# RWKV part of a hybrid layer: pair products in three lumps, filler blocks regrouped, the LoRA's low weights padded to 128 rows, the merge split by branch

## The chip, the cores and the metric

The kernel runs on one core of a Trainium2 chip. The metric is the device time of one execution in microseconds, median over several executions; the kernel before took 1315.39 us (median of 3, 1311.83 to 1317.93).

## The reference

One layer of a diffusion backbone, in fp32, for 512 latent tokens and 128 context tokens (640 in all, model width 1024). After a modulated RMS norm one wide projection gives the inputs of two branches and of two gates:

```python
h = _rmsnorm(x, p["norm1_g"]) * (1.0 + sc1) + sh1
u_rw, u_na, gate_rw, gate_na = jnp.split(h @ p["w_in"], IN_SPLITS, axis=-1)
o_rw, s_new = _rwkv_branch(u_rw, s0, ...)         # RWKV-7, both directions, 8 heads of 64
o_na = _na_latent(q, k, v, ctx_k, ctx_v, rpb)     # 2-D neighbourhood attention (context: plain attention)
merged = (jax.nn.sigmoid(gate_rw) * (o_rw @ p["w_o_rwkv"])
          + jax.nn.sigmoid(gate_na) * (o_na @ p["w_o_na"]))
x = x + g1 * (merged @ p["w_out"])
x = x + g2 * ((jax.nn.silu(h2 @ p["ffn_w1"]) * (h2 @ p["ffn_w3"])) @ p["ffn_w2"])
```

The RWKV branch is a recurrence over tokens, whose step is

```python
sa = jnp.einsum("bhvk,bhk->bhv", s, a)
s = s * w[:, :, None, :] + sa[..., None] * b[:, :, None, :] + v[..., None] * k[:, :, None, :]
y = jnp.einsum("bhvk,bhk->bhv", s, r)
```

with decay `w` and step size `a` made by small two-layer maps (the LoRAs). The outputs are both token groups after the layer, the new states, and the context's keys and values.

## The kernel before

The program runs in stages: modulation and norms; attention's projections and attention itself; the RWKV branch; the output projection; the feed-forward layer. The change touches the RWKV part, from about 285 to 770 us of the profile, and the first matmuls behind it.

**Precision.** A matrix product is done as three passes on TensorE: high weights on high activations, high on low, low on high. `wload` (L138) fetches a weight tile of 512 KB into `wst`, ScalarE casts the high part (`whi`, L149), and DVE or GpSimd subtracts it (`wlo`, L150). `feat_gen` (L158) issues the passes (L165) one after another, each of 128x320.

**Two kinds of work share TensorE.** RWKV is done in chunks of 64 tokens, for four pairs of heads (ct 0 to 3, `c` below), both directions. That work is many small matmuls (64x64 blocks, 32x32 in places) with waits on other engines between them. Into the waits the kernel puts *filler*: the matmuls of large projections that are needed anyway (tile `fl`), one by one from a generator (`stream`, L1264). The filler's units are the columns of the gate projections (`g0` to `g15`, 48 matmuls each), of keys, receptances and values of the next head pair (`k`, `r`, `v`, 48 each), and of the merge (`m0` to `m7`, 42 each: the 128 merged features of both branches, 4 K-tiles of attention and 3 of RWKV). `PRM["order"]` names their order, `wait` the marks that a unit needs. `PRM["plan"]` is a table with one entry per step of the small work: how many filler matmuls go in there, and how many steps of a second and third small generator. `weave` (L1294) reads it. TensorE's order is thus written out by hand; the other engines' order is set by a scheduler.

**One head pair** goes through these steps.
- `main` / `n_job` (L921): products of the chunk's keys and decayed keys (L931), in three groups of chunks (`parts8`: 8, 8 and 4), whose 32x32 corners ScalarE collects in `Nt`.
- `inv` (L1011): DVE transposes them into `RL` (L1015) and inverts 32x32 triangles of all chunks in place, in 30 steps ("hops", s = 1 to 30). A hop is a product into `pr` (L1043) and an add into `RL` (L1047), two of each; the first three and the last three use L1029 and L1036.
- In the hops, nine jobs on TensorE for the three groups, one at each third hop: `g_job` (Grams: 6 matmuls a chunk, into three PSUM buffers; DVE masks them into `AG`, L951, and `TG`, L954), `v_job` (values to token-major, or `flip` from the mirrored chunk, evicted by ScalarE), `t_job` (keys and decayed keys to token-major, two PSUM buffers, ScalarE). The six PSUM buffers with the tag `w` serve all small work in turn.
- Also there: `out` of the head pair before (group norm, with `inv_sqrt_bcast`: L874, DVE L878, GpSimd's power L880, ScalarE's copy L882, transposes L887; then bonus L1188, gate L1193) and `bonus` (L905).
- The blocks that complete 64x64 inverses: L1064 (32x32 matmuls), L1079.
- `carry` (L1088): eight chunks in sequence, three steps each: A (L1110, L1120, L1126), B (L1135, on the copy `x0` that ScalarE makes of A's result), C (L1147, L1151); then DVE makes the next state (L1164). Beside it the preparation of the next head pair (`prep_a`: the LoRA's pair of matmuls, L511 with 128 rows and L513 with 64, and more).

Attention's output `o` was written to DRAM in an earlier stage, the RWKV branch's is written head pair by head pair (L1204); `o_load` (L1212) brings back all seven K-tiles for the merge, 4 + 2 (or 3) K-tiles to a transfer. The merge multiplies by the gates, read back from DRAM (L1227), and sums (L1238, L1240). Its last K-tile, that of head pair 3, is never written: `last_gen` (L1361) multiplies it directly (L1372) and adds (L1373, L1375), and the output projection (`w0`) starts between its steps. The residual input `x2` (L1344) is loaded just before.

## Time and profile before

| | |
|---|---|
| median of 3 executions | 1315.39 us |
| profiled execution | 1312.36 us, its span 1310.5 us |
| TensorE busy | 1252.3 us, 96% of the span |
| DVE busy | 673.3 us, 51% |
| ScalarE, GpSimd busy | 468.1 us, 292.5 us |
| mean granted TensorE clock | 0.972 of 2.4 GHz |
| chain that ended last | TensorE 78%, DVE 13%, DMA 3% |

A profile covers one execution. Matmuls are pipelined, so their rows overlap, and the distance of two starts tells what one costs. The granted clock has two levels, 1.0 and 0.5 of full speed (2.4 and 1.2 GHz). A wait is put down to what came last.

### The profile page before, as it was taken

Reading aid. Unit: us, or ns where it says so; the run is one execution under the profiler, and the core shown is the slowest. Engines: PE = TensorE matmul, PEld = TensorE weight load, DVE = VectorE, ACT = ScalarE, POOL = GpSimd, SP = SyncE. Lnnn points to the kernel's source line nnn. Section 1 sums busy time; section 2 is a strip of 40 time slices with the busy share of each in tenths; the row PEclk is TensorE's granted clock in tenths of the full one; section 3 lists DMA queues with packets and bytes.
Section 4 is the critical chain, followed back from the end, with each engine's and each line's share of the span. In section 5 each row is a group of like instructions: output and inputs, shape, how many; then the busy total and the mean of one; then the engine's idle time right before and its main releaser. Section 6 shows DMA issues by size and latency. Waiting matters only on the chain.

```text
span 1310.5 us, 27065 instructions
## 1 busy us (share of the span) xinstructions
PE 1252.3 (96%) x11418; PEld 1081.0 (82%) x11418; DVE 673.3 (51%) x1458; ACT 468.1 (36%) x961; POOL 292.5 (22%) x292
## 2 busy tenths in 40 slices
...
GB/s 346 147 81 121 284 234 167 123 95 50 70 46 24 99 27 44 47 76 49 55 222 86 164 244 69 100 75 96 65 65 94 67 81 79 67 65 89 73 89 41
DMA packets 52849, 134.87 MB, mean 103 GB/s; under 512 B 6612, under 2 KB 20436, under 8 KB 50680
## 3 DMA queue, kind: packets, MB, share of 16 engines
...
## 4 chain that ended last, share of the span: by engine, by line
PE 78%; DVE 13%; DMA 3%; ACT 2%; issue 2%; POOL 1%; SPq 0%; DVEq 0%; ACTq 0%; POOLq 0%
PE f L165 24%; PE acc L252 21%; PE fl L165 12%; PE mm L165 4%; DVE pr L1043 3%; DVE RL L1047 3%; PE psa L203 2%; PE lg L756 1%; PE pt L704 1%; PE po L763 1%; PE w L1110 1%; DMA o<-o_d 1%; PE lg L755 1%; PE w L1135 1%; DVE AG L951 1%
## 5 line engine op out<-in xcount | busy, mean ns | idle before, releaser
L165 PE MATMUL f<-h,whi 128*128 128x256 f32 (+1 forms) x1408 | 306.3, 309 | 0.6 <-POOL h L155 0.6
L165 PEld LDWEIGHTS f<-h,whi 128*128 128x128 f32 x1408 | 236.6, 189 | 1.1 <-POOL h L155 1.0
L149 ACT CAST whi<-wst 128x1024 fp32r<-128x1024 f32 x126 | 132.0, 1049 | 274.6 <-PE acc L252 106.6
L165 PE MATMUL f<-h,wlo 128*128 128x384 f32 (+1 forms) x704 | 217.7, 309 | 0.0
L150 DVE TENSOR_TENSOR wlo<-wst,whi 128x1024 fp32r<-128x1024 f32 x95 | 117.9, 1243 | 180.1 <-ACT whi L149 180.0
L165 PE MATMUL fl<-h,whi 128*128 128x320 f32 x736 | 188.6, 334 | 0.0
L165 PEld LDWEIGHTS fl<-h,whi 128*128 128x128 f32 x736 | 129.5, 197 | 6.7 <-issue 0.2
L165 PEld LDWEIGHTS f<-h,wlo 128*128 128x128 f32 x704 | 133.0, 189 | 0.0
L165 PE MATMUL fl<-h,wlo 128*128 128x320 f32 x368 | 122.8, 334 | 0.0
L150 POOL TENSOR_TENSOR wlo<-wst,whi 128x1024 fp32r<-128x1024 f32 x31 | 83.6, 2698 | 106.4 <-ACT whi L149 102.7
L252 PE MATMUL acc<-whi,ul 128*128 128x512 f32 (+1 forms) x230 | 88.6, 385 | 0.0
L252 PE MATMUL acc<-whi,uh 128*128 128x512 f32 (+1 forms) x230 | 88.3, 386 | 0.0
L252 PE MATMUL acc<-wlo,uh 128*128 128x512 f32 (+1 forms) x230 | 88.2, 386 | 0.0
L252 PE MATMUL acc<-whi,h 128*128 128x512 f32 x240 | 80.7, 409 | 0.5 <-DVE h L361 0.5
L165 PEld LDWEIGHTS fl<-h,wlo 128*128 128x128 f32 x368 | 72.4, 197 | 3.8
L165 PE MATMUL fl<-o,whi 128*128 128x320 f32 x224 | 58.2, 338 | 14.2 <-DMA o<-o_d 12.6
L165 PE MATMUL mm<-h,whi 128*128 128x320 f32 x256 | 64.4, 329 | 0.0
L1490 DVE SCALAR_TENSOR_TENSOR a<-a,f 128x384 f32<-128x384 f32 (+1 forms) x44 | 21.5, 488 | 69.6 <-PE f L165 69.5
L252 PEld LDWEIGHTS acc<-whi,h 128*128 128x128 f32 x240 | 45.4, 191 | 14.0 <-issue 2.0
L165 PEld LDWEIGHTS fl<-o,whi 128*128 128x128 f32 x224 | 40.2, 200 | 17.0 <-DMA o<-o_d 13.4
L252 PE MATMUL acc<-whi,m 128*128 128x512 f32 x160 | 51.8, 400 | 0.0
L154 ACT CAST uh<-a 128x384 fp32r<-128x384 f32 (+1 forms) x44 | 20.2, 458 | 87.6 <-DVE a L1490 87.6
...
## 6 DMA issues: line engine op xcount, KB each, us to landing
...
```

The source lines that it names most:

```text
L149: act.copy(hi, st)
L150: (eng or dve).tensor_tensor(out=lo, in0=st, in1=hi.bitcast(F32), op=ALU.subtract)
L154: act.copy(hi, src)
L165: pe.matmul(ps[:, :t1 - t0], w[:, a:a + 128], x[:, k0 + kt, t0:t1], start=n == 0, stop=n == 3 * nk - 1)
L203: pe.matmul(ps[32 * j:32 * j + 32, c0:c0 + n], cs[:, kt, :], w[:, j * n:(j + 1) * n], start=kt == 0, stop=kt == 7)
L252: pe.matmul(pss[i][:, a:b], x[:, kt, ts_], w[:, cs_], start=ki == 0 and n == 0, stop=ki == last and n == 2)
L704: pe.transpose(pst[:, c * 128:(c + 1) * 128], L[:, c * 128:(c + 1) * 128], ident)
L755: pe.matmul(psl[:, o_:o_ + n], QS[hd][:, qs], KS[hd][:, k0:k0 + n], start=True, stop=False)
L756: pe.matmul(psl[:, o_:o_ + n], ql[rows, qs], KS[hd][rows, k0:k0 + n], start=False, stop=True)
L1043: dve.tensor_tensor(out=prv, in0=V(RL[:, s + 1 + a, :], [[32, b - a], [0, s]], s), in1=V(RL[:, s, :], [[0, b - a], [1, s]]), op=ALU.mult)
L1047: dve.tensor_tensor(out=dst, in0=dst, in1=prv, op=ALU.add)
L1490: dve.scalar_tensor_tensor(out=a, in0=a, scalar=0.5, in1=p3[:, :n], op0=ALU.mult, op1=ALU.mult)
```

## The change

- The nine jobs become three lumps, at hops 2, 9 and 16: each does the value, the transpose and the Gram job of one group.
- `plan` is new. The three groups of `n_job` run without filler between them, and filler goes in fewer, larger blocks. In `carry` none stands between steps A and B (the second of three places), 9 matmuls after B and 6 after C.
- The merge's units are split: `a0` to `a7` (attention's 4 K-tiles, 24 matmuls) and `b0` to `b7` (RWKV's 3, 18 matmuls), each with its own weight load of 512 or 384 columns and its own gate load (`merge_load`), in two buffers. `b` waits for the mark O2, `a4` to `a7` for the end of ct 3's `main`. `o_load` makes one transfer per K-tile.
- The LoRA's low weights lie in one persistent tile `UL` with zeros in the other 64 rows, so that L513's successor multiplies 128 rows.
- `inv_sqrt_bcast` yields once more between power and copy, and `out` may go on while `main` runs.

Outside the RWKV part TensorE's matmuls stand in the same order as before. The number of filler matmuls is 1440 in both, the number of uninterrupted blocks of them in the region 172 before and 105 now (counted in TensorE's order). The diff, cut:

```diff
@@ -26,40 +26,40 @@
 TCARGS = dict(schedule_with_timeline_sim=True)
 
 PRM = dict(
-    order=("g2 k1 g3 r1 g4 v1 g5 k2 g6 r2 g7 g8 v2 g9 k3 g10 r3 g11 v3 g12 g13 g14 g15 m0 m1 m2 m3 m4 m5 m6 "
-           "m7"),
+    order=("g2 k1 g3 r1 g4 g5 v1 g6 g7 k2 r2 g8 g9 v2 g10 g11 k3 r3 g12 g13 v3 g14 g15 a0 a1 a2 a3 a4 a5 a6 a7 "
+           "b0 b1 b2 b3 b4 b5 b6 b7"),
...
-        "16 2 2 2 6",
-        "0.0.0 6.0.1 5.0.1 4.0.1 5.0.1 5.0.0 5.1.0 5.0.0 5.1.0 4.0.0 5.1.0 5.0.0 5.1.0 5.0.0 4.1.0 5.0.0 "
-        "5.1.0 5.0.0 5.1.0 4.0.0 5.1.0 5.0.0 5.1.0 5.0.0 5.1.0 4.0.0 5.1.0 5.0.0 5.1.0 5.0.0 4.1.0 5.0.0 "
-        "8.1.0 8.0.0 7.1.0 4.0.0 4.1.0 4.0.0",
-        "9.0 4.1 4.1 5.1 4.1 5.1 4.1 4.1 5.1 4.1 4.1 5.1 4.1 4.1 5.1 4.1 5.1 4.1 4.1 5.1 4.1 4.1 5.1 4.1 4.1 "
-        "7.1",
...
+        "28.0 0.0 0.0 0.0 0.0",
+        "0.0.0 13.0.1 3.0.0 11.0.0 4.0.0 4.0.1 3.0.1 4.0.1 4.0.0 3.0.0 11.0.0 4.0.0 3.0.0 4.0.0 4.0.0 3.0.0 "
+        "4.0.0 11.0.0 4.0.0 3.0.0 4.0.0 4.0.0 3.0.0 4.0.0 3.0.0 4.0.0 4.0.0 3.0.0 4.0.0 4.0.0 3.0.0 4.0.0 "
+        "9.0.0 7.0.0 8.0.0 0.0.0 7.0.0 0.0.0",
+        "10.0 0.0 9.2 6.2 0.0 9.2 6.2 0.0 9.2 6.2 0.0 9.2 6.2 0.0 9.2 6.2 0.0 9.2 6.2 0.0 9.2 6.2 0.0 9.2 6.2 "
         "6.0",
...
+        "24.2 0.0 0.0 0.0 0.0",
+        "0.0.0 19.1.1 0.1.0 0.0.0 0.1.0 0.1.1 0.1.1 0.1.1 0.1.0 0.1.0 0.0.0 2.0.0 2.1.0 2.1.0 7.1.0 7.1.0 "
+        "7.1.0 7.0.0 7.0.0 7.0.0 7.0.0 7.0.0 7.0.0 7.0.0 7.0.0 7.0.0 7.0.0 7.0.0 7.0.0 7.0.0 7.0.0 7.0.0 "
+        "11.0.0 9.0.0 10.0.0 0.0.0 9.0.0 0.0.0",
+        "10.0 0.0 9.0 6.0 0.0 9.0 6.0 0.0 9.0 6.0 0.0 9.0 6.0 0.0 9.0 6.0 0.0 9.0 6.0 0.0 9.0 6.0 0.0 9.0 6.0 "
+        "6.0",
...
-    h3=1, h4=1.07, g1=2)
+    jobs=(2, 9, 16), h3=1, h4=1.07, g1=2)
...
@@ -143,11 +143,12 @@
             rot.append(rot.pop(0))
         pl, nst, nhl = rot[-1] if rot else wpool[-1]
         st = pl.tile([P, 1024], F32, tag="wst", bufs=nst, name=nm("wst"))
-        sp.dma_start(st if len(src.shape) == 2 else V(st[:, :], [[128, 8], [1, 128]]), src)
+        n = src.shape[1] if len(src.shape) == 2 else 1024
+        sp.dma_start(st[:, :n] if len(src.shape) == 2 else V(st[:, :], [[128, 8], [1, 128]]), src)
         hi = pl.tile([P, 1024], F32R, tag="whi", bufs=nhl, name=nm("whi"))
         lo = pl.tile([P, 1024], F32R, tag="wlo", bufs=nhl, name=nm("wlo"))
-        act.copy(hi, st)
-        (eng or dve).tensor_tensor(out=lo, in0=st, in1=hi.bitcast(F32), op=ALU.subtract)
+        act.copy(hi[:, :n], st[:, :n])
+        (eng or dve).tensor_tensor(out=lo[:, :n], in0=st[:, :n], in1=hi[:, :n].bitcast(F32), op=ALU.subtract)
         return hi, lo
...
@@ -414,6 +415,10 @@
     kt_ = kp.tile([P, NT], F32, tag="kt", bufs=1, name="kt_")
     vp0 = kp.tile([P, NT], F32, name="vp0")
 
+    UL = kp.tile([P, 2, 2, 128], F32R, name="UL")
+    for d in range(2):
+        pool.memset(UL[64 - 64 * d:128 - 64 * d, d].bitcast(F32), 0.0)
+
     def pre_t():
         return kp.tile([P, 643], F32, tag="pre", bufs=4, name=nm("pre"))[:, :NT]
 
-        S.ul = kp.tile([P, 2, 128], F32R, tag="ul", bufs=1, name=nm("ul"))
+        S.ul = UL
         act.copy(V(S.uh[:, 0, :], [[1, 512]]), upw[:, 0:512])
         for d in range(2):
             rr = hrows[d]
-            pool.tensor_tensor(out=S.ul[rr], in0=V(upw[rr, :], [[256, 2], [1, 128]], 128 * d),
+            pool.tensor_tensor(out=UL[rr, d], in0=V(upw[rr, :], [[256, 2], [1, 128]], 128 * d),
                                in1=V(S.uh[rr, d, :], [[256, 2], [1, 128]]).bitcast(F32), op=ALU.subtract)
 
     def parts(ct, k):
...
-                    pe.matmul(ps[:, :H2], S.ul[drows, wi, :], x[drows, hf * H2:(hf + 1) * H2],
+                    pe.matmul(ps[:, :H2], S.ul[:, d, wi, :], x[:, hf * H2:(hf + 1) * H2],
...
                               op1=ALU.add)
             pool.tensor_tensor(out=r, in0=r, in1=mhalf[:, :10], op=ALU.pow)
             yield
+            yield
             act.copy(c64(sqt), V(r[:, :], [[1, 10], [0, 64]]))
             yield
             pa, pb = ps_(), ps_()
...
-        jobs = {2 + 3 * i: (f, l) for i, (f, l) in enumerate(
-            (f, l) for l in parts8 for f in (g_job, v_job, t_job))}
+        jobs = dict(zip(PRM["jobs"], parts8))
...
-                    jobs[s][0](S, *jobs[s][1])
+                    for f in (v_job, t_job, g_job):
+                        f(S, *jobs[s])
                 yield
...
-            for t, t_d in zip(o, o_d):
-                sp.dma_start(t.bitcast(F32)[:, a:b, :], t_d[a:b, :, :].rearrange("q p t -> p q t"))
+            for q in range(a, b):
+                for t, t_d in zip(o, o_d):
+                    sp.dma_start(t.bitcast(F32)[:, q, :], t_d[q])
...
-        def mt_load(c8):
-            ts_ = pre_t(), pre_t()
-            for t, src in zip(ts_, (tna_d, trw_d)):
-                sp.dma_start(t, src[c8])
-            return ts_
-
-        def merge_gen(c8, w):
-
-            mt.append(mt_tile(c8))
-            ta, tr = mt_load(c8)
+        def merge_load(g, i):
+
+            k0, k1, src = (0, 4, tna_d) if g == "a" else (4, 7, trw_d)
+            w = wload(w_o[i][:, 128 * k0:128 * k1], pool)
+            t = sb.tile([P, NT], F32, tag="mx", bufs=2, name=nm("mx"))
+            sp.dma_start(t, src[i])
+            return w, t
+
+        def merge_gen(g, c8, wt):
+
+            w, t = wt
+            if g == "a":
+                mt.append(mt_tile(c8))
+            k0, nk = (0, 4) if g == "a" else (4, 3)
             for (a, b) in halves:
-                for (t, out_, nk, k0) in ((ta, mt[c8], 4, 0), (tr, tr, 3, 4)):
-                    ps = flps()
-                    yield from feat_gen(ps, w, o, nk, a, b, wcol=128 * k0, k0=k0)
-                    dve.scalar_tensor_tensor(out=out_[:, a:b], in0=t[:, a:b], scalar=1.0, in1=ps[:, :b - a],
-                                             op0=ALU.add, op1=ALU.mult)
-                pool.tensor_tensor(out=mt[c8][:, a:b], in0=mt[c8][:, a:b], in1=tr[:, a:b], op=ALU.add)
+                ps = flps()
+                yield from feat_gen(ps, w, o, nk, a, b, k0=k0)
+                dve.scalar_tensor_tensor(out=(mt[c8] if g == "a" else t)[:, a:b], in0=t[:, a:b], scalar=1.0,
+                                         in1=ps[:, :b - a], op0=ALU.add, op1=ALU.mult)
+                if g == "b":
+                    pool.tensor_tensor(out=mt[c8][:, a:b], in0=mt[c8][:, a:b], in1=t[:, a:b], op=ALU.add)
 
         def unit(g):
+
             i = int(g[1:])
-            if g[0] == "m":
-                return w_o[i], lambda w: merge_gen(i, w)
+            if g[0] in "ab":
+                return 24 if g[0] == "a" else 18, lambda: merge_load(g[0], i), lambda w: merge_gen(g[0], i, w)
             if g[0] == "g":
-                return w_rw[15 + i], lambda w: gate_gen(i, w, flps, sb, "fl")
+                return 48, lambda: wload(w_rw[15 + i], pool), lambda w: gate_gen(i, w, flps, sb, "fl")
             ci, dst = {"k": (4 + i, kt_), "r": (i, rt_), "v": (8 + i, v)}[g[0]]
-            return w_rw[ci], lambda w: proj_gen(ci, dst, flps, kp, "pre", 4, w)
+            return 48, lambda: wload(w_rw[ci], pool), lambda w: proj_gen(ci, dst, flps, kp, "pre", 4, w)
...
-        wait.update({f"m{i}": "O2" if i < 4 else "I3" for i in range(8)})
+        wait.update({f"a{i}": "A3" for i in range(4, 8)})
+        wait.update({f"b{i}": "O2" for i in range(8)})
...
-                        if i + 1 < len(order) and order[i + 1] == "m0":
-                            o_load(0, 4)
-                            o_load(4, 7 if "O2" in marks else 6)
+                        if i + 1 < len(order) and order[i + 1] == "a0":
+                            o_load(0, 6)
+                            if "O2" in marks:
...
-                weave(main(ct, S))
+                weave(main(ct, S), (og,))
+                marks.add(f"A{ct}")
```

On TensorE, at ct 1's `n_job` (`fl` is filler; lines of the second piece are those of the changed file: L931 is L936 there, L165 is L166), before:

```order
L165 MATMUL fl_4439<-h_85,whi_4173 128x320
L931 MATMUL w_4466<-AG,f_706_4380 32x64 x32
L165 MATMUL fl_4439<-h_86,whi_4173 128x320
L165 MATMUL fl_4439<-h_85,wlo_4174 128x320
L931 MATMUL w_4502<-AG,f_715_4432 32x64 x32
L165 MATMUL fl_4439<-h_85,whi_4173 128x320
L165 MATMUL fl_4439<-h_86,whi_4173 128x320
L931 MATMUL w_4538<-AG,f_706_4380 32x64 x8
L931 MATMUL w_4538<-AG,f_715_4432 32x64 x8
L165 MATMUL fl_4439<-h_85,wlo_4174 128x320
```

and now:

```order
L166 MATMUL fl_4528<-h_85,whi_4352 128x320
L936 MATMUL w_4546<-AG,f_696_4325 32x64 x32
L936 MATMUL w_4580<-AG,f_712_4424 32x64 x32
L936 MATMUL w_4614<-AG,f_696_4325 32x64 x8
L936 MATMUL w_4614<-AG,f_712_4424 32x64 x8
L166 MATMUL fl_4528<-h_86,whi_4352 128x320
L166 MATMUL fl_4528<-h_85,wlo_4353 128x320
```

The two filler blocks between the three groups are gone; behind them 16 filler matmuls stand in one block, and then the first lump.

On DVE, in ct 1's inverse (L1043 and L1047 are the hops; L951, L954 the masks of the first group's Grams), before:

```order
L1047 TENSOR_TENSOR RL_4566<-RL_4566,pr_4581 128x12x8
L1043 TENSOR_TENSOR pr_4581<-RL_4566 128x99 x2
L1047 TENSOR_TENSOR RL_4566<-RL_4566,pr_4581 128x11x9
L951 TENSOR_TENSOR AG<-w_4593,K 64x8x64 x2
L954 TENSOR_TENSOR TG<-w_4594,K 128x8x64
L1047 TENSOR_TENSOR RL_4566<-RL_4566,pr_4581 128x11x9
L954 TENSOR_TENSOR TG<-w_4595,K 128x8x64
```

and now (L956 and L959 are the masks, L1047 and L1051 the hops):

```order
L1047 TENSOR_TENSOR pr_4654<-RL_4632 128x119 x2
L1051 TENSOR_TENSOR RL_4632<-RL_4632,pr_4654 128x7x17 x2
L956 TENSOR_TENSOR AG<-w_4716,K 64x8x64 x2
L1047 TENSOR_TENSOR pr_4654<-RL_4632 128x108
L1047 TENSOR_TENSOR pr_4654<-RL_4632 128x126
L959 TENSOR_TENSOR TG<-w_4717,K 128x8x64
L959 TENSOR_TENSOR TG<-w_4718,K 128x8x64
L1051 TENSOR_TENSOR RL_4632<-RL_4632,pr_4654 128x6x18
```

The masks of the first Gram stood behind the hop of width 9 and stand behind the hop of width 17 now.

On SyncE's queue, at the end of the RWKV part (L1344 is `x2`, L146 a weight load, L1366 the gates for `last_gen`), before:

```order
L1227 DMA pre_8993<-tna_d 128x640
L1227 DMA pre_8994<-trw_d 128x640
L1344 DMA x_0_9112<-in_xs_dram 128x1024
L1344 DMA x_1_9113<-in_xs_dram 128x1024
L1344 DMA x_2_9114<-in_xs_dram 128x1024
L1344 DMA x_3_9115<-in_xs_dram 128x1024
L1344 DMA x_4_9116<-in_xp_dram 128x1024
L146 DMA wst_9130<-in_w_o_dram 128x8x128
L1227 DMA pre_9050<-tna_d 128x640
L1366 DMA tr_9158<-trw_d 128x640
L1366 DMA tr_9160<-trw_d 128x640
```

and now (L1359, L147, L1381 in the same roles; L1235 is `merge_load`):

```order
L147 DMA wst_9185<-in_w_o_dram 128x8x128
L1235 DMA mx_9001<-trw_d 128x640
L147 DMA wst_9191<-in_w_out_dram 128x1024
L1235 DMA mx_9067<-trw_d 128x640
L1381 DMA pre_9205<-trw_d 128x640
L1381 DMA pre_9207<-trw_d 128x640
L1381 DMA pre_9209<-trw_d 128x640
L147 DMA wst_9555<-in_w_out_dram 128x1024
L147 DMA wst_9603<-in_w_out_dram 128x1024
L1381 DMA pre_9211<-trw_d 128x640
L1359 DMA x_0_9167<-in_xs_dram 128x1024
L1359 DMA x_1_9168<-in_xs_dram 128x1024
```

The loads of `w_o`, of the first tile of `w_out` and of four gates stand ahead of `x2` now.

## Rows read from the trace of the kernel before

**Rows 1.** Stretches: length, busy time of PE, PEld, DVE, ACT, POOL; clock, DMA:
```profile
297.00:340.00 43.00, 42.45 (x811) 38.30 (x801) 38.94 (x133) 18.27 (x36) 18.31 (x16) 1.00 0.18 57
...
393.00:443.50 50.50, 46.80 (x845) 41.71 (x844) 42.96 (x141) 21.75 (x44) 15.02 (x18) 1.00 0.16 52
...
509.00:562.50 53.50, 47.98 (x837) 43.21 (x836) 40.84 (x140) 21.93 (x44) 14.90 (x17) 0.94 0.18 60
...
620.50:684.00 63.50, 47.99 (x805) 42.00 (x803) 41.68 (x142) 17.79 (x33) 17.67 (x13) 0.82 0.40 143
```

**Rows 2.** TensorE's waits, 285 to 770 us: total, times, longest:
```profile
PE fl L165 <- DMA o<-o_d: 12.6, 3, 5.8
PE w L887 <- ACT pre L882: 5.7, 4, 2.1
...
PE fl L1372 <- DVE pre L1373: 4.0, 1, 4.0
```

**Rows 3.** TensorE in time, filler (start, length, instruction):
```profile
290.30 0.46 PE L165 MATMUL fl<-h,whi 128*128 128x320 f32 x2
...
290.74 0.46 PE L165 MATMUL fl<-h,whi 128*128 128x320 f32 x2
...
447.18 0.73 PE L165 MATMUL fl<-h,whi 128*128 128x320 f32 x2
...
447.98 0.73 PE L165 MATMUL fl<-h,whi 128*128 128x320 f32 x2
```

**Rows 4.** TensorE in time, ct 3's carry:
```profile
715.51 0.45 PE L1120 MATMUL w<-ZV,K 64*64 64x64 f32 x8
715.79 0.40 PE L1126 MATMUL w<-R__2920,ZV 64*64 64x64 f32 x8
716.12 0.42 PE L165 MATMUL fl<-o,wlo 128*128 128x320 f32 x1
...
716.91 0.45 PE L1135 MATMUL w<-x,Rt 64*64 64x64 f32 x8
```

**Rows 5.** TensorE in time, ct 1's carry, a LoRA pair:
```profile
468.54 0.31 PE L511 MATMUL w<-lx,uh 128*128 128x320 f32 x1
...
469.13 0.69 PE L1147 MATMUL w<-ZV,TG 128*64 128x64 f32 x16
```

**Rows 6.** TensorE in time, ct 0's last chunk, steps A and B without filler:
```profile
388.32 0.45 PE L1126 MATMUL w<-R__2920,ZV 64*64 64x64 f32 x8
388.80 0.45 PE L1135 MATMUL w<-x,Rt 64*64 64x64 f32 x8
```

**Rows 7.** DVE in time, ct 1's inverse:
```profile
398.67 1.25 DVE L1015 STREAM_TRANSPOSE RL<-Nt 128x1024 f32<-128x1024 f32 x1 [3.01 <-ACT Nt L934]
...
405.41 1.39 DVE L951 TENSOR_TENSOR AG<-w,K 64x512 f32<-64x512 f32 x2
...
414.70 0.46 DVE L1043 TENSOR_TENSOR pr<-RL 128x112 f32<-128x112 f32 x2
...
415.47 0.47 DVE L1043 TENSOR_TENSOR pr<-RL 128x120 f32<-128x120 f32 x2
```

**Rows 8.** Further stretches, columns as in rows 1:
```profile
443.00:446.40 3.40, 3.40 (x86) 3.16 (x85) 3.33 (x7) 1.42 (x4) 1.76 (x2) 1.00 0.19 44
446.40:449.80 3.40, 3.40 (x18) 3.07 (x18) 1.48 (x4) 1.90 (x4) 1.15 (x1) 0.50 0.36 139
...
508.90:512.50 3.60, 3.60 (x165) 2.95 (x164) 0.00 (x0) 2.14 (x2) 1.55 (x1) 1.00 0.37 123
```

**Rows 9.** The chain of waits, 650 to 690 us (start, length, piece):
```profile
659.50 9.86 DMA o<-o_d
```

**Rows 10.** The end of the RWKV part, engines in time:
```profile
739.32 0.77 PE L887 MATMUL w<-K,pre 128*128 128x128 f32 x5 [0.16 <-ACT pre L882]
...
744.37 2.32 DVE L155 TENSOR_TENSOR o<-out,o 128x320 fp32r<-128x320 f32 x1
```

**Rows 11.** The chain of waits, 740 to 790 us:
```profile
769.34 0.60 DVE pre L1373 x2
```

37 lines of the change are left out of this document (15 added, 22 removed).

## The prediction

> **What bounds the kernel now.** I read the page first, then the RWKV part by stretches, then TensorE's waits there, then TensorE and DVE row by row. TensorE is the engine to watch: in ct 1's `n_job` and inverse it is busy 46.80 of 50.50 us [rows 1]. The exception is ct 3, 47.99 of 63.50 us at a mean clock of 0.82 [rows 1], where filler waits 12.6 us for `o` to come back from DRAM [rows 2]. The other waits are short: 5.7 us for the copy in `out`'s inverse square root, 4.0 us at the first matmul of the last step [rows 2]. So two things can move the time: what TensorE's own instructions cost, and the waits.
>
> A filler matmul costs 0.147 us in a run of its kind: three from 290.30 to 290.74. At the lower clock it is 0.267: 447.18 to 447.98 [rows 3]. A block of filler costs more than its matmuls. In `carry` four fill 716.12 to 716.91, 0.79 us instead of 0.59, so 0.20 is paid where 64-row work follows. The eight small matmuls ahead take 0.33 us to the filler (715.79 to 716.12), where eight of that kind before small work take 0.28 [rows 4]: 0.05 more. A block between small matmuls thus costs 0.25 us beside its work.
>
> **The change part by part.**
>
> *Filler blocks.* 172 become 105, with 1440 matmuls in both. 67 x 0.25 = 16.8 us less. Where 128-row work follows, the surcharge should be smaller. No row here isolates it; with 0.10, half the smaller value, 67 blocks give 6.7, and with 0.30 they give 20.1. I take 0.25, from the row.
>
> *LoRA.* A pair takes 468.54 to 469.13, 0.59 us [rows 5]. The second matmul has 64 rows and is followed by small work. With 128 rows both run at filler's pace and only one switch is left, 0.147 + 0.147 + 0.20 = 0.49. 24 pairs x 0.10 = 2.4 us less. From both sides: nothing gained, or, if the switch hides, 24 x 0.30 = 7.1. The Trainium skill ("TensorE: Matmul & The Clock Gate", Step-by-step: what each phase is for) says that the time goes by the columns streamed, not by the rows. By it 128 rows would save nothing and the sum would be 2.4 us smaller. The row's pair costs twice what two 320-column matmuls cost in a run, which speaks for a cost of the switch that this rule does not name.
>
> *No filler between steps A and B.* I cost it at nothing. B waits for the copy `x0` of A's first matmuls, and the matmuls L1120 and L1126 of A still cover it: in ct 0's last chunk, without filler, B starts 0.48 us after the start of the last eight of A, whose length is 0.45 [rows 6]. If ScalarE is late, each of 32 chunks pays: 0.3 us each would be 10 us. The 9 and 6 filler matmuls in the other two places cover B's copies and DVE's new state, 1.3 and 0.9 us where before four or five matmuls gave 0.6 to 0.7; what waits for the state they save I leave out.
>
> *Lumps.* This is the part that adds waits. A lump takes all six `w` buffers, and the next user of a buffer waits until the masks have run; DVE has them later in its order. In ct 1, `RL` begins at 398.67, and the first Gram's masks began 6.7 us later, behind hop 9 [rows 7]. A hop costs 0.77 there (414.70 to 415.47), so the eight hops to the 17th add 6.2, and the masks take 1.39 [rows 7]: they now end 14.3 us after the start of `RL`, which itself waits for ScalarE's copy of `n_job`. TensorE has until there 38 filler matmuls (5.6 us), the first lump, and a bonus, two steps of `out` and three blocks' surcharges (about 1.7, at 0.147 and 0.25). A lump is 192 instructions as the trace counts them (an fp32 matmul twice), and 165 such ran in 3.60 us [rows 8], so 4.2 us. That is 11.5 of 14.3, and TensorE waits about 3 us. The second lump waits in the same way, for buffers that `bonus` and `out` hold until hops 23 to 26 are through: I take 5 more. So 8 us in ct 1 and in ct 2, and 6 in ct 0, where no `out` stands between. Before, the stretches had 0.6, 3.7 and 5.5 us without a matmul in ct 0, 1 and 2 [rows 1]. That is 5.4 + 4.3 + 2.5 = 12.2 more. In return `out`'s inverse square root has one more step and more filler to hide in, so two of its four waits go, 3.6 of the 5.7 us [rows 2]. Net +8.6. Bounds: nothing, if the filler covers the masks; 24 if the waits are twice as long.
>
> *ct 3.* The `o` loads are asked for as 12 transfers instead of 4, one K-tile each, and early filler (`a0`) needs the first K-tiles alone. Before, a transfer of 9.86 us ended the wait [rows 9], and the RWKV K-tile of ct 2 came after it; `a` units don't need that one. I let 5 of 12.6 us stand. On the other side the second bonus waits behind all hops of ct 3 with almost no filler ahead of it, about 12 us, since the attention units come after it. `out`'s longest wait, 2.1 us [rows 2], goes. Before, 15.5 us of the stage had no matmul, and a mean clock of 0.82 means 23 us at the lower level, part of them idle [rows 1]: some 24 us lost in all. I set 18 now: 6 less. Bounds: all 24 stay, or 10 more go with the second bonus.
>
> *The end.* Before, all filler left over ran after the last gate, and covered what leads from `out`'s transposes to the last step, 739.32 to about 745 [rows 10]. Now nothing is left there: 5.6 us with 1.1 us of work, a wait of 4.5. What it replaces is as long: TensorE waited 4.0 us [rows 2], since DVE had `w_out` ahead of it and started the step at 769.34 [rows 11]. On SyncE that weight now stands ahead of `x2`. I take +0.5. The last step itself is bound by DVE in both.
>
> *Clock and the rest.* Falls after the 32x32 blocks, as from 446.40 [rows 8], cost 3.4 us x (1 - 0.147 / 0.267) = 1.5 each; I let one stand per head pair, about as many as now. The weights of the merge come in smaller pieces on SyncE and GpSimd, of the same bytes: nothing.
>
> Sum: -16.8 - 2.4 + 8.6 - 6 + 0.5 = -16.1 us. Against the profiled execution, 1312.36, whose span is 1310.5, that is 1296.3. The median shown, 1315.39, lies 3.0 above that execution; I forecast 1299 for a median.
>
> **The rivals.**
>
> *The waits eat it.* If lumps wait so much longer that they cost 12.2 more, and ct 3 keeps its 24 us (6 more), the sum is +2.1: about 1317. For it: each of the waits is on DVE, which is busy 42.96 of 50.50 us in that stage [rows 1], and a wait that DVE makes longer shifts its own later masks. Against: filler is bigger at those places.
>
> *The clock falls after lumps.* Slower. Granted clock fell to 0.50 from 446.40 to 449.80, right behind L1064, though TensorE was busy for all of the 3.4 us before [rows 8]. Lumps are the same sort of work, 4.2 us of small blocks, and `n_job` without filler in front of them makes 8. If each lump, each `n_job` and each of the two blocks at the inverse's end, 24 in four head pairs, brought such a stretch, 24 x 1.5 = 36 us, less the 6 that stand already: 1299 + 30 = 1329. It decides from 11 stretches more on (16.1 / 1.5). Against: 165 small matmuls from 508.90 to 512.50 ran at 1.00 [rows 8]. The Trainium skill ("TensorE: Matmul & The Clock Gate", Why this matters for your kernels) asks only that TensorE has no idle gaps. By that rule lumps would cost nothing, and idle waits would; the fall at 446.40 without any gap speaks against the rule as the whole story.
>
> *More than that.* If `o` is there in time and the second bonus finds its buffer, 10 us of ct 3's 18 go: 1289.
>
> *It does not do what it says.* Blocks that cost 0.10 and no gain of the LoRA: -6.7 + 8.6 - 6 + 0.5 = -3.6: about 1312.
>
> **How the numbers follow.** The forecast has 0.50 (1292 to 1306), more than that 0.16, the waits 0.14, the cheap blocks 0.07, the clock 0.13. A difference of 0.5%, 6.6 us, is about what a measurement tells from none. Faster by more than that: 0.50 + 0.16 and a small part of the two in between, 0.70. Slower: the clock, most of its share, 0.12. Same: 0.18. The range reaches from the greater gain to where the waits have eaten it, 1284 to 1317.
>
> **What would show it.** Right: 105 blocks, each still 0.2 to 0.3 us dearer than its matmuls; the wait for `o` down to about 5 us; no wait left at L892, the old L887, in ct 1 and ct 2; new waits of L910 and L996 for masks and bonuses on DVE, some 8 us in a head pair; the last step's first product on DVE at about 753 instead of 769. Wrong: a granted clock of 0.5 behind most lumps; waits at L1140, the old L1135, for `x0` in most chunks; or waits on DVE of over 12 us in ct 0 to 2.

## The result and the profile after

The changed kernel took 1320.03 us (median of 13 runs, 1315.01 to 1324.74), the kernel before 1313.25 beside it: a ratio of 1.0044, 95% interval 1.0029 to 1.0059. It is 6.8 us slower where 16 less were forecast. Its profiled execution took 1320.28 us, span 1318.3, against 1312.36 and 1310.5.

The page of the changed kernel, span and busy times:

```profile
span 1318.3 us, 27127 instructions
...
PE 1238.9 (94%) x11418; PEld 1087.6 (83%) x11418; DVE 669.2 (51%) x1458; ACT 466.8 (35%) x969; POOL 292.7 (22%) x302
```

TensorE is busy 13.4 us less than before (1252.3), and the span is 7.8 longer: TensorE stands idle 21.2 us more. So the saved work is there, and the waits took more than it gave.

TensorE's waits in the changed kernel, 285 to 790 us (total, times, longest; they answer to [rows 2]). L910 is the bonus's matmul, L996 and L951 are matmuls of a lump, L1140 is step B, L1115 step A, L892 `out`'s transposes, L1387 the last step:

```profile
PE w L910 <- DVE AG L956: 18.4, 3, 8.1
PE w L1140 <- ACT x L1135: 6.1, 8, 1.0
PE w L1115 <- DVE ZV L1169: 6.0, 4, 1.9
PE fl L166 <- DMA o<-o_d: 4.9, 2, 3.8
PE w L996 <- DVE AG L956: 3.9, 1, 3.9
PE fl L166 <- DVE mt L1247: 3.5, 2, 2.0
PE fl L166 <- ACT U L450: 3.1, 1, 3.1
PE fl L1387 <- ACT o L155: 2.8, 1, 2.8
...
PE w L892 <- ACT pre L887: 1.7, 1, 1.7
```

The wait for `o` fell from 12.6 to 4.9 us and L892 waits once, at the end. New on top are the waits for masks (`AG`), and below them step B's for `x0`. Step A's wait for the new state is not new. It was 4.9 us and is 6.0; before:

```profile
PE w L1110 <- DVE ZV L1164: 4.9, 8, 1.2
```

Stretches of the changed kernel, columns as in [rows 1]: first `n_job` and inverse of ct 0 to 3, then parts of ct 1 and ct 2:

```profile
295.10:343.30 48.20, 41.11 (x798) 38.90 (x797) 42.96 (x140) 16.94 (x34) 14.18 (x14) 0.89 0.13 43
407.30:462.10 54.80, 47.70 (x821) 44.07 (x820) 43.26 (x146) 20.80 (x42) 18.01 (x14) 0.88 0.14 47
525.30:581.10 55.80, 46.07 (x823) 42.94 (x822) 43.58 (x142) 17.74 (x35) 10.16 (x12) 0.88 0.13 42
644.60:709.10 64.50, 48.51 (x826) 44.57 (x825) 42.98 (x151) 16.68 (x32) 12.23 (x15) 0.84 0.38 134
...
412.00:417.00 5.00, 4.31 (x194) 3.98 (x193) 4.89 (x28) 3.17 (x5) 0.75 (x6) 1.00 0.02 7
421.90:425.40 3.50, 0.42 (x3) 0.09 (x1) 3.46 (x13) 0.77 (x2) 3.50 (x1) 0.99 0.00 0
425.40:435.60 10.20, 10.20 (x138) 9.48 (x139) 10.16 (x51) 0.43 (x1) 2.39 (x4) 0.50 0.16 53
530.00:535.00 5.00, 4.24 (x194) 3.90 (x193) 4.89 (x14) 3.45 (x6) 3.11 (x9) 1.00 0.18 49
540.90:544.80 3.90, 0.00 (x0) 0.00 (x0) 3.90 (x22) 0.19 (x1) 0.00 (x0) 1.00 0.00 0
544.80:558.50 13.70, 10.07 (x131) 9.38 (x135) 10.15 (x49) 1.36 (x3) 1.97 (x1) 0.50 0.01 2
```

In ct 0, 1 and 2 TensorE has 7.1, 7.1 and 9.7 us without a matmul (length less busy time), 23.9 in all against 9.8 before. The clock is 0.88 to 0.89 where it was 1.00, 1.00 and 0.94.

The last six rows show two of the falls. A first lump runs at 1.00 (412 to 417, 530 to 535), then TensorE waits for masks. In ct 1 the wait is 3.08 us, and the next 10.2 us are at 0.50, though TensorE is busy for all of them. In ct 2 it is 8.1 us; the clock falls 4.5 us into it (544.8) and stays at 0.50 for 13.7 us. Two other falls, at 346.8 and 712.0 for 3.5 us each, stand behind no wait but behind the 80 matmuls of 32x32 of L1069, with TensorE busy for 3.4 us ahead of each.

From 282 us, where a stretch at 0.50 begins, to 790 TensorE was busy 66.2 us at the lower level, 41.6 before (added up over the stretches at 0.50). At 0.147 us against 0.267 for the same matmul [rows 3], the 24.6 more cost 24.6 x 0.45 = 11.1 us.

Single instructions of the changed kernel in time (start, length, engine, line, what):

```profile
371.30 2.96 POOL L151 TENSOR_TENSOR wlo<-wst,whi 128x1024 fp32r<-128x1024 f32 x1
...
372.06 2.88 DVE L595 SCALAR_TENSOR_TENSOR f<-NK,pre 128x640 f32<-128x640 f32 x1
374.87 0.60 DVE L1169 TENSOR_TENSOR ZV<-w,Dt 64x128 f32<-64x128 f32 x2
...
375.20 0.77 PE L1115 MATMUL w<-ZV,AG 128*64 128x64 f32 x8 [0.90 <-DVE ZV L1169]
...
411.33 1.25 DVE L1019 STREAM_TRANSPOSE RL<-Nt 128x1024 f32<-128x1024 f32 x1 [7.31 <-ACT Nt L939]
412.61 1.35 DVE L1033 SCALAR_TENSOR_TENSOR RL<-RL 128x30 f32<-128x30 f32 x6
...
423.80 1.39 DVE L956 TENSOR_TENSOR AG<-w,K 64x512 f32<-64x512 f32 x2
...
478.56 0.32 PE L515 MATMUL w<-lx,uh 128*128 128x320 f32 x1
478.72 0.30 PE L517 MATMUL w<-lx,UL 128*128 128x320 f32 x1
478.86 0.31 PE L515 MATMUL w<-lx,uh 128*128 128x320 f32 x1
479.00 0.31 PE L517 MATMUL w<-lx,UL 128*128 128x320 f32 x1
479.24 0.69 PE L1115 MATMUL w<-ZV,AG 128*64 128x64 f32 x16
...
530.61 3.48 DVE L1033 SCALAR_TENSOR_TENSOR RL<-RL 128x30 f32<-128x30 f32 x6
...
531.31 2.36 POOL L151 TENSOR_TENSOR wlo<-wst,whi 128x1024 fp32r<-128x1024 f32 x1
...
546.89 1.39 DVE L956 TENSOR_TENSOR AG<-w,K 64x512 f32<-64x512 f32 x2
...
752.13 0.41 PE L166 MATMUL fl<-o,wlo 128*128 128x320 f32 x1
...
753.65 0.45 PE L1152 MATMUL w<-ZV,TG 128*64 128x64 f32 x8
...
768.04 0.76 PE L892 MATMUL w<-K,pre 128*128 128x128 f32 x5 [1.66 <-ACT pre L887]
...
772.66 0.94 PE L1387 MATMUL fl<-o,whi 128*128 128x320 f32 x2 [2.77 <-ACT o L155]
...
773.87 0.49 DVE L1388 SCALAR_TENSOR_TENSOR pre<-pre,fl 128x320 f32<-128x320 f32 x1 [0.33 <-PE fl L1387]
```

Three things are to be seen. A LoRA pair ahead of small work takes 0.38 us (478.86 to 479.24), where it took 0.59 [rows 5]. A block of nine filler matmuls takes 1.52 us (752.13 to 753.65), nine times 0.147 and 0.20 on top, as in [rows 4]. And at 372.06 a product on DVE lasts 2.88 us beside GpSimd's subtraction for a filler weight (L151): the state is late by it, and step A waits 0.90 us. The three other waits for the state, 5.1 us, have the same sign, such a subtraction beside a DVE product. One of them:

```profile
388.02 2.38 POOL L151 TENSOR_TENSOR wlo<-wst,whi 128x1024 fp32r<-128x1024 f32 x1
...
388.10 2.98 DVE L904 SCALAR_TENSOR_TENSOR bv<-bv,D,rt__612 128x640 f32<-128x640 f32 x1 [2.15 <-POOL bv L605]
```

L904 takes 0.87 us at 626.41, where no subtraction begins ahead of it.

### The profile page after: what moved, and what is told of

Its sections match the earlier page's. It is cut to its first block, busy times and chain, and to the rows that moved or that the text cites. A ratio compares the mean times of both kernels' runs of the same rounds, so it can differ in the third digit from the quotient of the medians.

```text
span 1318.3 us, 27127 instructions
## 1 busy us (share of the span) xinstructions
PE 1238.9 (94%) x11418; PEld 1087.6 (83%) x11418; DVE 669.2 (51%) x1458; ACT 466.8 (35%) x969; POOL 292.7 (22%) x302
## 4 chain that ended last, share of the span: by engine, by line
PE 79%; DVE 13%; ACT 3%; issue 2%; POOL 1%; DMA 1%; SPq 0%; ACTq 0%; DVEq 0%; POOLq 0%
PE f L166 24%; PE acc L253 21%; PE fl L166 13%; PE mm L166 4%; DVE pr L1047 2%; PE psa L204 2%; DVE RL L1051 2%; PE lg L760 1%; PE po L767 1%; PE pt L708 1%; PE lg L759 1%; PE w L1115 1%; PE w L1069 1%; PE w L1084 1%; PE w L1140 1%
## 5 line engine op out<-in xcount | busy, mean ns | idle before, releaser
L166 PE MATMUL f<-h,whi 128*128 128x256 f32 (+1 forms) x1408 | 306.3, 309 | 0.6 <-POOL h L156 0.6
L166 PEld LDWEIGHTS f<-h,whi 128*128 128x128 f32 x1408 | 236.6, 189 | 1.1 <-POOL h L156 1.0
L150 ACT CAST whi<-wst 128x1024 fp32r<-128x1024 f32 (+2 forms) x134 | 132.5, 992 | 279.0 <-PE acc L253 108.7
L166 PE MATMUL f<-h,wlo 128*128 128x384 f32 (+1 forms) x704 | 217.6, 309 | 0.0
L151 DVE TENSOR_TENSOR wlo<-wst,whi 128x1024 fp32r<-128x1024 f32 x95 | 118.9, 1254 | 178.4 <-ACT whi L150 178.4
L166 PE MATMUL fl<-h,whi 128*128 128x320 f32 x736 | 183.3, 333 | 3.1 <-ACT U L450 3.1
L166 PEld LDWEIGHTS fl<-h,whi 128*128 128x128 f32 x736 | 128.9, 198 | 9.5 <-ACT U L450 3.4
L166 PEld LDWEIGHTS f<-h,wlo 128*128 128x128 f32 x704 | 133.0, 189 | 0.0
L166 PE MATMUL fl<-h,wlo 128*128 128x320 f32 x368 | 118.2, 321 | 0.0
L151 POOL TENSOR_TENSOR wlo<-wst,whi 128x1024 fp32r<-128x1024 f32 (+2 forms) x39 | 81.5, 2089 | 120.2 <-ACT whi L150 111.2
L166 PEld LDWEIGHTS fl<-h,wlo 128*128 128x128 f32 x368 | 72.5, 197 | 1.0
L166 PE MATMUL mm<-h,whi 128*128 128x320 f32 x256 | 63.9, 327 | 0.4 <-ACT pre L523 0.4
L166 PE MATMUL fl<-o,whi 128*128 128x320 f32 x224 | 55.0, 330 | 8.4 <-DMA o<-o_d 4.9
L166 PEld LDWEIGHTS mm<-h,whi 128*128 128x128 f32 x256 | 44.0, 193 | 8.8 <-issue 7.1
L253 PEld LDWEIGHTS acc<-whi,ul 128*128 128x128 f32 x230 | 43.2, 188 | 9.6
```

The source lines that it names most:

```text
L150: act.copy(hi[:, :n], st[:, :n])
L151: (eng or dve).tensor_tensor(out=lo[:, :n], in0=st[:, :n], in1=hi[:, :n].bitcast(F32), op=ALU.subtract)
L166: pe.matmul(ps[:, :t1 - t0], w[:, a:a + 128], x[:, k0 + kt, t0:t1], start=n == 0, stop=n == 3 * nk - 1)
L253: pe.matmul(pss[i][:, a:b], x[:, kt, ts_], w[:, cs_], start=ki == 0 and n == 0, stop=ki == last and n == 2)
```

## Experiments

All were timed beside the kernel before. Ratios are to it, with the 95% interval. Differences in the text are of medians. The kernel before came out between 1310.9 and 1313.3 us in the five series, highest beside the change, so differences to the change are about 2 us smaller by the ratios: 14.8 for 16.6, 6.6 for 8.7, 22.4 for 25.0, 10.0 for 12.1 and 9.1 for 11.6.

| kernel | median, us | ratio |
|---|---|---|
| the change | 1320.03 | 1.0044 [1.0029, 1.0059] |
| inv_as_before | 1303.43 | 0.9931 [0.9918, 0.9945] |
| carry_as_before | 1311.35 | 0.9994 [0.9974, 1.0013] |
| merge_split_only | 1304.51 | 0.9952 [0.9933, 0.9971] |
| lora_pad_only | 1307.69 | 0.9965 [0.9950, 0.9980] |
| lora_and_split | 1294.93 | 0.9882 [0.9857, 0.9907] |
| carry_alone | 1296.18 | 0.9885 [0.9863, 0.9907] |
| covered_lumps | 1295.07 | 0.9873 [0.9852, 0.9893] |
| covered_lumps_old_carry | 1314.86 | 1.0032 [1.0015, 1.0050] |
| two_covers | 1286.56 | 0.9802 [0.9778, 0.9825] |
| old_carry_longer_cover | 1308.26 | 0.9977 [0.9963, 0.9992] |
| half_cover | 1307.96 | 0.9968 [0.9953, 0.9984] |
| same_phase | 1308.44 | 0.9975 [0.9961, 0.9990] |

In all but lora_pad_only and merge_split_only the lines behind the plan stand some 12 lower than in the changed kernel: its L166 is L154 there, L910 L898, L951 L939, L996 L984, L1140 L1128, L1115 L1103.

### The parts by themselves

**inv_as_before**: the changed kernel with the nine jobs, and before's plan for `main` and the inverse; carry, LoRA and merge stay changed.

```diff
-        jobs = dict(zip(PRM["jobs"], parts8))
+        jobs = {2 + 3 * i: (f, l) for i, (f, l) in enumerate(
+            (f, l) for l in parts8 for f in (g_job, v_job, t_job))}
...
-        "28.0 0.0 0.0 0.0 0.0",
+        "16 2 2 2 6",
```

> The changed kernel with the main and inverse stages as before: nine jobs at every third hop, the old filler table for those stages, one yield less in the inverse square root. Carry table, padded LoRA and split merge stay. Theory W (the lumps' masks on DVE come too late, TensorE waits and its clock falls): the four stages from n_job to the end of the inverse took 223.3 us after and 210.9 before, though they hold 25 filler matmuls (3.7 us) less, so this gives back about 16 us: 1304, some 9 below before, and the second bonus waits for no mask (18.4 us after). Theory C (the uncovered step from A to B in carry is what costs): no change against the changed kernel, 1320. Theory B (a filler block costs nothing, so nothing was saved): 1313, as before.

16.6 us less than the changed kernel: theory W holds. The lumps as they are placed cost more than the blocks of filler they save.

**carry_as_before**: the changed kernel with before's carry rows in the plan.

```diff
-        "10.0 0.0 9.2 6.2 0.0 9.2 6.2 0.0 9.2 6.2 ...
+        "9.0 4.1 4.1 5.1 4.1 5.1 4.1 4.1 5.1 4.1 ...
```

> The changed kernel with the old filler table in carry (three blocks a chunk of 4, 4 and 5), the rest changed. Theory W: carry's regrouping saves some 11 us of block surcharges (0.25 us each and the filler it takes out of later stages is only moved) and gives back 6.1 us in waits for x0 and 2 or 3 more for the state and the clock, so undoing it costs 2 to 6 us: 1323. Theory C: undoing it gains the 12 us of waits: 1308. In both the waits for x0 (6.1 us in eight places after) go to under 0.5.

8.7 us less, which is nearer theory C's time, but not where theory C put it. The four carries took 211.1 us with 614 filler matmuls, against 210.5 with 609 in the changed kernel: the waits for `x0` are gone, and the smaller blocks cost as much. The four stages from `n_job` to the end of the hops took 214.4 us against 223.3 with the same filler, most of it in ct 1 (47.9 against 54.8), where the bonus waits 1.3 us for masks instead of 3.1 and the filler's wait of 3.1 us for `U` is gone. In all 13.3 of the 18.4 us of the bonus's waits (L898 here) stay. So this run does not show that the regrouping itself loses time; it shifts which filler matmul each inverse starts with.

**merge_split_only**: before with the merge split by branch and the finer `o` loads; **lora_pad_only**: before with the padded low weights; **lora_and_split**: both.

```diff
-                    pe.matmul(ps[:, :H2], S.ul[drows, wi, :], x[drows, hf * H2:(hf + 1) * H2],
+                    pe.matmul(ps[:, :H2], S.ul[:, d, wi, :], x[:, hf * H2:(hf + 1) * H2],
...
-            for t, t_d in zip(o, o_d):
-                sp.dma_start(t.bitcast(F32)[:, a:b, :], t_d[a:b, :, :].rearrange("q p t -> p q t"))
+            for q in range(a, b):
+                for t, t_d in zip(o, o_d):
+                    sp.dma_start(t.bitcast(F32)[:, q, :], t_d[q])
```

> The kernel before with the merge split by branch, one transfer per K-tile of o, and nothing else changed. Theory W: the wait for o goes from 12.6 to about 5 us and the end's wait for w_out goes, while the order at the end keeps its filler: 5 to 10 us faster, 1306. Rival: o was waited for because DMA is full then (1.0 of 16 engines from 660 us), and the split changes only who waits: 1313.

> The kernel before with the LoRA's low weights padded to 128 rows, nothing else. A pair took 0.59 us before, and 0.39 alone or 0.34 in groups of two in the changed kernel's trace. If the difference is the switch between 128 and 64 rows: 24 pairs x 0.20 = 4.8 us faster, 1308. If it comes from how pairs are grouped, or the time goes by columns alone: 1313.

> The kernel before with the padded LoRA weights and the split merge, no other change. If the two parts add: 1311.7 - 7.2 - 4.0 = 1300.5. If the carry regrouping of the run inv_as_before (1303.4, the same two parts with carry regrouped) saves its blocks, this is slower than that, up to 1308; if regrouping costs its waits, this is the faster one.

Both gain, 0.48% and 0.35% (6.3 and 4.6 us), as theory W of the split and the switch of the LoRA had said, and together 1.2% (15.5 us). That is more than their sum of 10.9, but at the edge of what the intervals tell. TensorE's wait for `o` in merge_split_only, against 12.6 us before [rows 2]:

```profile
PE fl L154 <- DMA o<-o_d: 5.2, 4, 3.6
```

Where the other 4.6 us of the pair come from, if they are more than noise, was not settled. Its time at the lower clock, idle time included, is 41 us, as with the split alone (54.6 before). Against inv_as_before, which has the same two parts with the change's carry rows, the pair is 8.5 us faster.

**carry_alone**: lora_and_split with the carry's filler in two blocks a chunk and none between A and B, the count in each chunk unchanged (156 blocks instead of 186).

> Padded LoRA, split merge and carry's filler in two blocks a chunk, none between A and B, with the same number of filler matmuls and the same places of the preparation steps as before: 156 blocks for 186. Theory W: 30 x 0.25 = 7.5 us less for the blocks, 4 to 6 us more for waits on x0, so 1 to 4 us below the run with LoRA and split alone. Theory C (the uncovered step costs more than the block): 0 to 6 us above it. If a block costs only 0.1: 3 us less and the same waits, so 1 to 3 above it.

No difference to lora_and_split: thirty blocks fewer pay for the wait that the missing filler leaves at step B. So the uncovered step alone does not account for the 8.5 us of inv_as_before, whose carries of ct 0 to 2 also hold more filler (142 matmuls each, 103 to 127 in these two). In carry_alone:

```profile
PE w L1127 <- ACT x L1122: 6.7, 8, 1.6
```

### Lumps with something ahead of their waits

**covered_lumps**: the changed kernel; in each inverse 35 to 50 filler matmuls move from behind the last lump to behind the first, ahead of the bonus. TensorE's small work is in the same order. As the generator hands out no filler while a unit waits for its mark, 9, 3 and 18 of the matmuls do not run in the inverses of ct 0 to 2 any more but behind the last of them, in ct 3's carry. **half_cover** moves half as many.

```diff
-        "0.0.0 13.0.1 3.0.0 11.0.0 4.0.0 ...
+        "0.0.0 13.0.1 3.0.0 46.0.0 4.0.0 ...
```

> The changed kernel with filler moved inside each inverse stage, from behind the third lump to between the first lump and the bonus (35, 35 and 50 matmuls in ct 0 to 2, 45 before the second bonus in ct 3), the number of blocks and of matmuls unchanged. Theory W: TensorE has 5 to 7 us more work until the first masks are done, the 22 us of waits for AG masks fall to 3 to 6, and with them the half-clock stretches that followed each of them: 1300 to 1306. Rival (the clock falls because of the lumps' small matmuls): waits go but 10 us stretches at 0.5 stay behind lumps: 1310 or more. Rival (DVE is what bounds the stage): the wait comes back before L1069: 1317 to 1320.

> The changed kernel with half of the move of the covered kernel: 18, 18, 25 and 22 filler matmuls from behind the lumps to between the first lump and the bonus (the covered kernel: 35, 35, 50 and 45; its time 1295 against 1320 without). Theory W: the waits for the masks shrink by what is put ahead of them, about half of 22 us stays, and the time is about halfway: 1304 to 1311. Rival K (what counts is that TensorE's clock falls once it waits at all, however briefly): at least one wait is left in each stage, the half-clock stretches stay at about 70 us in all, and the time is 1314 to 1321.

25.0 us less with the whole cover, more than was expected, and 12.1 with half of it. That the half came out at half is luck: the whole cover also shifts what the carries start with, and half_cover does not (its carries of ct 0 to 2 take 52.8, 53.1 and 54.7 us). The section on the carry takes the two apart. Rival K's time is refuted, though the time at half clock stays at 65 us there, near its 70. The waits of the bonus for the masks (18.4 us) are gone with the whole cover; these remain:

```profile
PE w L939 <- DVE bv L899: 9.1, 2, 8.8
PE w L984 <- DVE bv L899: 8.7, 2, 5.3
```

They are the second lump, which needs the bonus's PSUM tile. **two_covers** moves 34, 34 and 26 matmuls more, to between bonus and second lump:

```diff
-        "0.0.0 13.0.1 3.0.0 46.0.0 4.0.0 4.0.1 3.0.1 4.0.1 4.0.0 3.0.0 ...
+        "0.0.0 13.0.1 3.0.0 46.0.0 4.0.0 4.0.1 3.0.1 4.0.1 4.0.0 37.0.0 ...
```

> The covered kernel with a second move of filler in ct 0 to 2: 34, 34 and 26 matmuls from behind the second and third lump to between the bonus and the second lump, where TensorE still waited 9.1, 5.3 and 3.5 us (17.9 in all) for VectorE's product that empties the bonus's PSUM tile behind the hops. Theory W (a lump's time is lost only where TensorE's fixed order puts nothing ahead of a product that VectorE makes late): these waits fall under 5 us, the half-clock stretches around them go, and the time falls from 1295 to 1278 to 1286. Rival D (VectorE's chain of hops is the bound of the inverse stages by now): the waits move to the third lump or to the first product of the next carry, and the time stays at 1292 to 1298.

1286.56 us, 2% below the kernel before and the best version found. The gain is 8.5 us, just short of the 9 to 17 expected, and lies in the inverses of ct 0 to 2 (145.9 us before the second move, 138.7 with it). lora_and_split, with none of the lumps, had 1294.93, so the lumps and the new plan bring nothing over it with one cover and 8.4 us with two; which share the lumps have in these and which the plan was not separated. Of the 17.8 us for `bv` this is left:

```profile
PE w L984 <- DVE bv L899: 0.3, 1, 0.3
```

### Why the same carry takes 53 us or 48

The carries of ct 0 to 2 took 52.8, 53.1 and 53.5 us in the changed kernel (from one stage's first matmul to the next stage's), and 48.1, 48.1 and 50.6 in covered_lumps, with the same instructions of TensorE in the same order. What differs is which filler matmul a carry starts with. **same_phase** leaves the lumps without cover and only takes 9, 3 and 18 filler matmuls from the end of the three inverses, so that the carries start as in covered_lumps.

> The changed kernel with 9, 3 and 18 filler matmuls fewer behind the lumps of ct 0, 1 and 2 (they run behind the last carry instead), and no move of cover: each carry of ct 0 to 2 then starts with the same filler matmul as in the covered kernel (235, 571 and 892 done), whose carries took 48.1, 48.1 and 50.6 us where those of the changed kernel took 52.8, 53.1 and 53.5 with the same instructions of TensorE. Theory G (what makes the difference is where the filler's weight loads fall, ScalarE's cast ahead of the copy x0 and GpSimd's subtraction beside DVE's work ahead of the new state): the carries take 48 to 51 us, the waits at L1140 and L1115, 12.1 us in the changed kernel, fall under 6, and with the masks' waits as they are the time is 1307 to 1313. Rival M (the carries suffer from the late masks before them, by what these delay on DVE and ScalarE): the carries stay at 52 to 54 and the time is 1317 to 1321, up to 2 us less for what is moved.

The carries took 48.1, 48.1 and 50.6 us, 12.6 less in all, the time fell by 11.6 us, and rival M is refuted. The other stages moved as well: `n_job` and inverse of ct 0 to 2 took 148.2 us instead of 158.8, with 30 filler matmuls less, that of ct 3 took 71.6 instead of 64.5, and the last carry ran the 30. Step A's waits for the state are gone, and those for `x0` are 3.4 us. The place that was late at 372.06 in the changed kernel, in same_phase:

```profile
369.91 0.83 DVE L583 SCALAR_TENSOR_TENSOR f<-NK,pre 128x640 f32<-128x640 f32 x1
...
369.99 2.97 POOL L139 TENSOR_TENSOR wlo<-wst,whi 128x1024 fp32r<-128x1024 f32 x1 [0.80 <-ACT whi L138]
...
370.65 0.60 DVE L1157 TENSOR_TENSOR ZV<-w,Dt 64x128 f32<-64x128 f32 x2
```

DVE starts 0.08 us ahead of GpSimd and takes 0.83 us. In the changed kernel GpSimd started 0.76 us ahead, and DVE's product ended 0.68 us behind it. The Trainium skill ("SBUF — State Buffer", SBUF: two separate sides) says that a DVE operation with two SBUF inputs and a GpSimd operation that reads SBUF share a pair of ports, that the first to start holds it for its whole instruction, and that the other stands still. Both traces agree, with 2.88 and 0.83 us for the same product. GpSimd's 2.96 us in the changed kernel fit too: DVE's product before (370.67 to 372.03) was running when it began.

For the state theory G thus holds, at all four waits. For `x0` it is shown in part. Of the seven waits of 0.7 to 1.0 us in the changed kernel one had a weight's cast ahead of the copy on ScalarE (368.75), one the eviction of a projection, and five the preparation of the next head pair (L570, L583). Three waits of this last kind, 3.4 us, are what same_phase has left.

covered_lumps and same_phase have the same filler in every stage and differ by the cover alone, by 13.4 us. TensorE's work at half clock between 285 and 790 us is 37.8 against 62.1 us, which makes 10.9 of them. By stage, ct 3's inverse took 57.7 us instead of 71.6, those of ct 0 to 2 together 145.9 instead of 148.2: there the waits for masks had only become waits for `bv`, and two_covers brought the gain.

**covered_lumps_old_carry** is covered_lumps with before's carry rows, **old_carry_longer_cover** that with 45 matmuls more in ct 3's cover.

> As covered_lumps, with carry's filler as in the kernel before. If the 8.7 us that the old carry table gave back in the changed kernel belong to carry: 8 below covered_lumps, 1292 to 1298. If they came from another position of the filler's units in the inverse stages: within 3 us of covered_lumps.

> The covered kernel with before's carry plan (measured 1314.9, with ct 3's stage up to H at 70.3 us against 57.7 with the changed carry plan), and 45 filler matmuls more in ct 3 ahead of the second lump, taken from the last carry. With before's carry plan 45 fewer are used up by then, so that the first merge matmul, which waits for the loads of o, comes behind the second lump and not ahead of it. Theory S (the wait for o and the wait for the masks then stand one behind the other; beside each other the longer one counts): the o wait is back ahead of the second lump, the stage takes 62 to 66 us with 207 filler matmuls, the last carry loses 7 to 10 us with its 45, and the time falls to 1298 to 1305. Rival B (before's carry plan costs this much by its own blocks and order): 1312 to 1318, since the carries are the same as in the kernel with 1314.9.

The first came out 20 us above covered_lumps, which neither theory had. Before's carries use 45 filler matmuls fewer, so ct 3's cover ends before the first matmul that needs `o`. Two stretches of ct 3 in covered_lumps_old_carry, from the cover's end to the second lump's, then the merge:

```profile
642.70:657.90 15.20, 9.40 (x203) 7.86 (x201) 11.33 (x47) 3.51 (x6) 3.19 (x2) 0.66 0.10 29
657.90:674.60 16.70, 9.29 (x33) 6.55 (x29) 3.46 (x6) 1.31 (x3) 2.08 (x2) 0.69 0.82 293
```

and in covered_lumps, from the first wait for `o` to the end of cover, then bonus and second lump:

```profile
641.30:653.70 12.40, 7.28 (x20) 5.18 (x21) 11.78 (x57) 0.80 (x2) 4.17 (x1) 0.63 0.94 344
653.70:661.00 7.30, 7.23 (x206) 6.33 (x205) 3.20 (x6) 3.40 (x6) 0.86 (x1) 0.92 0.05 16
```

Where the loads of `o` and DVE's hops run in the same 12.4 us, one low-clock stretch pays for both. From the cover's first matmul to the third lump, with the same small work and as many filler matmuls in both, it is 38.8 us where they come one behind the other (635.87 to 674.65) and 28.5 where they coincide (637.03 to 665.50). The longer cover brought 6.6 us where 10 to 17 were expected. The masks' wait is gone, but `o` alone is waited for longer, 8.9 us:

```profile
PE fl L154 <- DMA o<-o_d: 8.9, 4, 8.0
```

So theory S explains a part. The other 13 us to covered_lumps lie in ct 3 and in the carries, whose filler blocks are 24 instead of 16 there; they were not separated further.

## Why the prediction was wrong

The sum was -16.1 us and the span changed by +7.8. By kinds of time, in the profiled executions:

| | forecast | measured |
|---|---|---|
| TensorE's work at full clock | -16.8 - 2.4 = -19.2 | -13.4 - 11.1 = -24.5 |
| work at half clock | 0 | +11.1 |
| TensorE idle | +8.6 - 6 + 0.5 = +3.1 | +21.2 |

The half-clock figure is that of the RWKV part. Over the whole spans it is 78.9 against 57.8 us, so +9.5, and the first row -22.9. Of the idle time +14.2 lies in the inverses of ct 0 to 2, +0.5 in that of ct 3, +6.5 in the carries of ct 0 to 2, and about none in the rest together.

- **Filler blocks and LoRA: right, the LoRA too small.** The surcharge is still 0.20 us behind a block. The LoRA was forecast at 2.4 us with 0.49 for a pair; at 0.38 it is 24 x 0.21 = 5.0, and lora_pad_only gained 4.6. Taken from the -22.9, that leaves 17.9 for the blocks, close to the 16.8.
- **No filler between A and B: this step failed.** I costed it at nothing and named the case against it, ScalarE late in each chunk. The wait for `x0` came in 8 of 32 chunks (6.1 us, and 6.7 in carry_alone), and the one for the new state, which I had left out as a gain, went from 4.9 to 6.0. I had not asked what stands ahead of those copies: for the state GpSimd's subtractions of filler weights beside DVE's products, for `x0` mostly ScalarE's preparation of the next head pair, and once a cast. Where the subtractions fall depends on how many filler matmuls the inverse has used. With another start the same carries were 12.6 us shorter (same_phase).
- **Lumps: the idle time was about right, its consequence was not.** 6, 8 and 8 us without a matmul were forecast, 7.1, 7.1 and 9.7 came. In ct 1 that is partly luck: 3.1 us of it are filler that waits for ScalarE's `U` (L450), and the second lump's 5 us did not come. ct 2 is longest: DVE's L1033 took 3.48 us there (1.35 in ct 1), with a weight's subtraction on GpSimd beginning 0.7 us behind its start, and the masks stand four hops later in DVE's order, 3.0 us more. The sum took `out`'s two waits off twice: 1.5 and 1.9 of the 3.6 us lie in the 3.7 and 5.5 us without a matmul that it had already subtracted, so +8.6 should have read about +12. What I left out is that a wait brings a stretch at 0.50 behind it: "I let one stand per head pair, about as many as now" is the second step that failed, 11.1 us. covered_lumps shows the price, 10.9 us less at half clock than same_phase.
- **ct 3: -6 did not come.** The wait for `o` fell to 4.9 us as I had said, and the second bonus waits (7.2 us of the 18.4 at L910, about 12 forecast); with the merge's own waits (3.5) 16.0 us are without a matmul, against 15.5.
- **The end: right.** A wait of 4.5 us was forecast between `out` and the last step; it is 1.7 + 2.8. It begins later only because all before it is late: DVE's first product is at 773.87 instead of 753.
- **The clock rival: refuted as I had put it.** The lumps themselves ran at 1.00. Most falls came behind waits, which is what the Trainium skill's rule that idle gaps bring the clock down would give ("TensorE: Matmul & The Clock Gate", Why this matters for your kernels); the rows from 412 to 435.6 agree. The fall at 446.40 in the kernel before [rows 8] had no such gap, and neither had those at 346.8 and 712.0 here, behind the first block at the inverse's end in ct 0 and ct 3. For that block the rival was right in two head pairs of four, and why the clock falls there stays open.

The mechanism of the rival "the waits eat it" is the nearest to what happened, with the clock's share on top and the carry's collisions beside it.
